# Routed experts: weight pieces of 512 columns, gate and linear columns in separate steps, second products two steps behind

## The chip, the core and the metric

The kernel runs on one core of a Trainium2 chip. The metric is the device time of one execution, in microseconds (us); it is given as the median of three runs. Five engines run their own instruction streams: PE (TensorE, matrix products), ACT (ScalarE), DVE (VectorE), POOL (GpSimd) and SP (SyncE, which here issues the large transfers). They wait for each other through semaphores. PEld is PE's loading of the stationary operand. The transfers of all queues share 16 DMA engines.

## The reference

Two layers on 512 tokens of width 1024: a state-space mixer with a dense SwiGLU, then an attention layer with eight routed SwiGLU experts, of which each token uses two. The change touches the experts alone:

```python
def _swiglu(x, w_in, w_out):
    g, u = jnp.split(x @ w_in, 2, axis=-1)        # w_in: 1024 x 7168, gate columns, then linear columns
    return (jax.nn.silu(g) * u) @ w_out           # w_out: 3584 x 1024

def _moe_swiglu(x, w_router, w_in, w_out):
    logits = (xf @ w_router).astype(jnp.float32)
    top_val, top_idx = lax.top_k(logits, TOP_K)   # two of eight experts per token
    gate = jax.nn.softmax(top_val, axis=-1)
    ...
    # each expert's tokens are gathered, go through _swiglu, and are added back times their gate
```

The layer ends with `LayerNorm(ALPHA * x + experts)`.

## The kernel before

The stage of the experts follows the router. The eight experts are ranked by how many tokens chose them; the code is built for fixed token counts by rank ("caps": 160, 148, 136, 132, 132, 128, 116, 112 in the version that runs here). Phases of one or two ranks follow each other: 4, then 0 and 7, then 1 and 6, then 3, then 2 and 5. Within a phase of two the chunks of both alternate; the last ten chunks of the stage are all of rank 5.

An expert's 3584 hidden columns are cut into 14 **chunks** of 256, so the stage has 112 chunks. A chunk needs three **pieces** of weights of 1 MB each, as float32: its 256 gate columns of the first matrix (all 1024 rows), its 256 linear columns, and its 256 rows of the second matrix. In memory a row's 256 columns are a run of 1 KB; a row of the second matrix is a run of 4 KB. `moe_load` issues the pieces from SP in the order gate, linear, second matrix, into six buffers `mraw`; the two pieces of the first chunk go into the two halves of `X`, which is free by then (`ahead`).

All products are made of float16 pairs. `moe_conv` has ACT write the high half of a piece (L1127), `moe_lo` has DVE write the low half (L1133) and then, since the buffer is free, issues the load six pieces later. The halves go to `wi` (first matrix, two buffers) or `woh`/`wol` (second matrix, three). `mm3` turns each product into three matmuls: high by high (L277), high by low (L278), low by high (L279).

A step `i` of the loop in `moe` has `moe_in(i, 0)` and `moe_in(i, 1)`, which make 128 columns each of the hidden width: eight row blocks times gate and linear, three matmuls each, in one bank of PSUM (`gu`, three banks). ACT makes `hs` = silu(gate) from the bank (L1150), DVE multiplies by the linear half (`hf`, L1151), rounds to `hh` (L1154) and subtracts for `hl` (L1155). Then `moe_out(i - 1)` multiplies the previous chunk's `hh`, `hl` with its second matrix into `y`. Per chunk that is 96 matmuls of cap columns for the first matrix, and for the second 48 of cap columns, or 12 of 512 columns where the cap is at most 128.

Between these, `fill` slips in pieces of other work: the gathering of the next phase's tokens (`dispatch`, L1077), the places of the rows (`where`), the transposed results of finished experts (`moe_rows`), and, in the last chunks, `moe_sum`: POOL loads the accumulated rows back from `XD` (L1232, four transfers of 512 KB, and one gather L1234), and the layer norm of all rows begins, shared by ACT, DVE and POOL (`STEPS`). `finish` adds the last expert and writes out. [...]

At the stage's beginning SP reads eight registers from `order` (L2205), the experts' numbers, then issues the first two pieces. While these load, PE gathers the first expert's tokens. POOL loads the gamma and beta of the last layer norm, broadcast to all partitions (`load_gb(1, 1)`, 512 KB written by each of two transfers).

## Time and profile before

| | |
|---|---|
| median of three runs | 1831.0 us (1829.42 to 1831.13) |
| the profiled execution, its own time | 1829.31 us |
| its span (first to last instruction) | 1827.5 us |
| PE busy / PEld busy | 1686.7 us / 1324.2 us |
| DVE busy / ACT busy / POOL busy | 1393.8 / 1003.0 / 220.5 us |
| moved by DMA over the span | 433.69 MB, 237 GB/s |

The stage of the experts runs from about 777 us to 1804 us of the span. "Busy" counts the time in which an engine has an instruction under way; matmuls overlap, so a busy PE need not be at its peak. The mean granted clock of TensorE over the span was 0.965 of full speed.

### The profile page before, as it was taken

Reading aid. Unit: us, or ns where it says so; the run is one execution under the profiler, and the core shown is the slowest. Engines: PE = TensorE matmul, PEld = TensorE weight load, DVE = VectorE, ACT = ScalarE, POOL = GpSimd, SP = SyncE. Lnnn points to the kernel's source line nnn. Section 1 sums busy time; section 2 is a strip of 40 time slices with the busy share of each in tenths; the row PEclk is TensorE's granted clock in tenths of the full one; section 3 lists DMA queues with packets and bytes.
Section 4 is the critical chain, followed back from the end, with each engine's and each line's share of the span. In section 5 each row is a group of like instructions: output and inputs, shape, how many; then the busy total and the mean of one; then the engine's idle time right before and its main releaser. Section 6 shows DMA issues by size and latency. Waiting matters only on the chain.

```text
span 1827.5 us, 45045 instructions
## 1 busy us (share of the span) xinstructions
PE 1686.7 (92%) x19531; PEld 1324.2 (72%) x19531; DVE 1393.8 (76%) x2049; ACT 1003.0 (55%) x1100; POOL 220.5 (12%) x232
## 2 busy tenths in 40 slices
PE   4689999999999888879999999999999999999974
PEld 4455464444445554579999999999999899999863
DVE  9873653333246685569999999999999899999987
ACT  4223333232232573267767766767777677777771
POOL 6920100000000200100000012120000100000125
PEclk7889999999999999789999999999999999999997
DMA  4236423432342000199999999999999999999991
GB/s 82 53 96 220 128 70 93 115 93 93 119 144 93 24 24 15 44 357 379 361 343 340 354 357 355 347 359 347 379 368 364 303 373 378 371 384 376 369 361 62
DMA packets 359320, 433.69 MB, mean 237 GB/s; under 512 B 30480, under 2 KB 321384, under 8 KB 359104
## 3 DMA queue, kind: packets, MB, share of 16 engines
q1 hardware_dynamic: 346832, 417.55, 67.2%
q0 software_dynamic: 3984, 12.56, 2.4%
q8 instruction: 156, 2.56, 0.6%
q10 hardware_dynamic: 8288, 0.54, 0.3%
q14 instruction: 60, 0.49, 0.1%
HBM read 416.81 MB, written 11.17 MB: 234 GB/s over the span
## 4 chain that ended last, share of the span: by engine, by line
PE 71%; DVE 16%; DMA 5%; ACT 4%; issue 3%; POOL 1%; SPq 0%; DVEq 0%; ACTq 0%; POOLq 0%
PE gu L277 9%; PE gu L279 9%; PE gu L278 9%; PE ps L278 7%; PE ps L279 7%; PE ps L277 7%; PE y L277 5%; PE y L279 5%; PE y L278 5%; DVE wi L1133 4%; DMA mraw<-in_moe_w_in_dram 3%; DVE wol L1133 2%; DMA mraw<-in_moe_w_out_dram 2%; PE glu L279 1%; PE glu L277 1%
## 5 line engine op out<-in xcount | busy, mean ns | idle before, releaser
L279 PE MATMUL gu<-xe,wi 128*128 128x132 f16 (+6 forms) x3584 | 635.4, 222 | 21.9 <-DVE wi L1133 21.8
L277 PE MATMUL gu<-xe,wi 128*128 128x132 f16 (+6 forms) x3584 | 635.5, 222 | 8.9 <-ACT wi L1127 4.5
L278 PE MATMUL gu<-xe,wi 128*128 128x132 f16 (+6 forms) x3584 | 635.4, 221 | 0.0
L1133 DVE SCALAR_TENSOR_TENSOR wi<-mraw,wi 128x2048 f16<-128x2048 f32 x222 | 507.3, 2285 | 5.9 <-ACT wi L1127 5.5
L1127 ACT ACTIVATE wi<-mraw 128x2048 f16<-128x2048 f32 x222 | 419.1, 1906 | 63.4 <-DMA mraw<-in_moe_w_in_dram 58.7
L279 PEld LDWEIGHTS <-wi 128*128 128x128 f16 x3584 | 350.3, 98 | 24.3 <-DVE wi L1133 24.2
L278 PEld LDWEIGHTS <-wi 128*128 128x128 f16 x3584 | 352.7, 98 | 9.5 <-issue 4.9
L277 PEld LDWEIGHTS <-wi 128*128 128x128 f16 x3584 | 350.8, 98 | 8.5 <-ACT wi L1127 4.7
L1133 DVE SCALAR_TENSOR_TENSOR wol<-mraw,woh 128x2048 f16<-128x2048 f32 x112 | 255.8, 2284 | 0.3 <-ACT woh L1127 0.3
L1127 ACT ACTIVATE woh<-mraw 128x2048 f16<-128x2048 f32 x112 | 213.5, 1906 | 22.9 <-DMA mraw<-in_moe_w_out_dram 22.6
L278 PE MATMUL y<-hl,woh 128*128 128x132 f16 (+3 forms) x1120 | 209.5, 225 | 0.0
L279 PE MATMUL y<-hh,wol 128*128 128x132 f16 (+3 forms) x1120 | 209.5, 225 | 0.0
L277 PE MATMUL y<-hh,woh 128*128 128x132 f16 (+3 forms) x1120 | 209.4, 225 | 0.0
L1150 ACT ACTIVATE hs<-gu 128x132 f32<-128x132 f32 (+4 forms) x224 | 62.2, 278 | 195.5 <-PE gu L279 195.3
L105 DVE SCALAR_TENSOR_TENSOR wf<-raw,wf 128x2048 f16<-128x2048 f32 x34 | 77.8, 2292 | 95.7 <-ACT wf L104 95.7
L277 PE MATMUL ps<-xt,wf 128*128 128x512 f16 x320 | 121.3, 379 | 0.0
L278 PE MATMUL ps<-xt,wf 128*128 128x512 f16 x320 | 121.3, 379 | 0.0
L279 PE MATMUL ps<-xt,wf 128*128 128x512 f16 x320 | 121.3, 379 | 0.0
L1185 POOL DMA_INDIRECT XD<-yr,at x12 | 24.8, 2066 | 787.8 <-ACT yr L1218 438.1
L277 PEld LDWEIGHTS <-woh 128*128 128x128 f16 x1120 | 109.6, 98 | 0.0
L279 PEld LDWEIGHTS <-wol 128*128 128x128 f16 x1120 | 109.6, 98 | 0.0
L278 PEld LDWEIGHTS <-woh 128*128 128x128 f16 x1120 | 109.5, 98 | 0.1
(471 smaller groups left out, 2746.7 us busy)
## 6 DMA issues: line engine op xcount, KB each, us to landing
mraw<-in_moe_w_in_dram SPq DMA_DIRECT2D x222, 1024.0 KB
mraw<-in_moe_w_out_dram SPq DMA_DIRECT2D x112, 1024.0 KB
raw<-in_ffn_w_in_dram SPq DMA_DIRECT2D x44, 512.0 KB
raw<-in_ffn_w_out_dram SPq DMA_DIRECT2D x11, 1024.0 KB
raw<-in_s_w_glu_dram SPq DMA_DIRECT2D x64, 128.0 KB
raw<-in_mla_o_w_dram SPq DMA_DIRECT2D x4, 1024.0 KB
XD<-X SPq DMA_DIRECT2D x5, 512.0 KB
xj<-in_x_dram SPq DMA_DIRECT2D x4, 512.0 KB
```

The costliest lines, as they stand in the source:

```text
L105: nc.vector.scalar_tensor_tensor(lo[:, c], raw[:, c], scale[j], hi[:, c], op0=OP.mult, op1=OP.subtract)
L277: mm(out, lh, rh, start=first, stop=False, **kw)
L278: mm(out, lh, rl, start=False, stop=False, **kw)
L279: mm(out, ll, rh, start=False, stop=last, **kw)
L1127: nc.scalar.activation(hi, raw, AF.Copy, scale=WS)
L1133: self.nc.vector.scalar_tensor_tensor(lo, raw, WS, hi, op0=OP.mult, op1=OP.subtract)
L1150: nc.scalar.activation(sg, p[:, :cap], AF.Silu, scale=1.0 / (WS * XS))
L1185: self.nc.gpsimd.indirect_dma_start(out=self.XD, out_offset=bass.IndirectOffsetOnAxis(ap=self.at[:n, j:j + 1], axis=0), in_=yr[:n], in_off ...
```

## The change

Two neighbouring chunks of an expert now share their weights' columns differently. `MOE` lists pairs: entry `(r, 2c)` is a step for the **gate** columns of 512 hidden columns, `(r, 2c + 1)` one for the **linear** columns. A piece of the first matrix is 512 columns by half of the 1024 rows (runs of 2 KB, still 1 MB); a piece of the second matrix is as before.

- `moe_in(i, half)` makes 256 columns of one kind in one bank. In a gate step ACT writes silu of two caps' width into `hs` and keeps it. In the linear step DVE makes `hf`, `hh`, `hl` of that width. The number and shape of the matmuls stay.
- The second matrix's pieces come one step later in the order of loads and conversions (`piece`), and `moe_out(i - 2)` takes the place of `moe_out(i - 1)`, except at the end of the last phase's two parts.
- The second matrix has four buffers: two tiles `wo` and the two halves of `X`.
- At the beginning SP reads one register, issues the first two pieces, and reads the other seven afterwards. The two pieces of the second step are issued ahead of the first piece of the second matrix; `moe_load(9)` issues all six buffers' loads at once (before: `moe_load(6)`, four).
- `load_gb(1, 1)` moves from the router to the first step of `moe_sum`.

```diff
-MOE = [rc for ph in PLAN for rc in sorted(((r, c) for c in range(NCH) for r in ph),
-       key=...)]
+MOE = [(r, 2 * c + v) for ph in PLAN for r, c in sorted(((r, c) for c in range(NCH // 2) for r in ph),
+       key=...)
+       for v in range(2)]
...
-            self.load_gb(1, 1)
...
             if part < 2:
-                nc.sync.dma_start(t.rearrange("p (k f) -> p k f", k=KD),
-                                  wi[:, bass.ds(e, 1), :, part, c * CH:(c + 1) * CH].rearrange("p o k f -> p (o k) f"))
+                n, k = 2 * CH, KD // 2
+                nc.sync.dma_start(t.rearrange("p (k f) -> p k f", k=k),
+                                  wi[:, bass.ds(e, 1), part * k:(part + 1) * k, c % 2, c // 2 * n:(c // 2 + 1) * n]
+                                  .rearrange("p o k f -> p (o k) f"))
...
+    def piece(self, i, part):
+
+        i -= part == 2
+        return (i if 0 <= i < NE * NCH else None), part
...
-    def moe_in(self, i, ft):
+    def moe_in(self, i, half):
...
+        for part in range(2):
+            for a in range(2):
+                for k in range(kh):
+                    s = k * 2 * CH + (2 * half + a) * 128
...
+                    self.mm3(p[:, a * cap:(a + 1) * cap], wih[:, part, s], wil[:, part, s], xh[:, kk], xl[:, kk],
+                             kk == 0 and a == 0, kk == KD - 1, skip_group_check=True)
...
+        if c % 2 == 0:
+            sg = self.hp.tile([128, w], F, name="hs", tag="hs", bufs=4)[:, :2 * cap]
+            nc.scalar.activation(sg, p[:, :2 * cap], AF.Silu, scale=1.0 / (WS * XS))
+            self.sg[i + 1, half] = sg
+            return
...
-        self.mh[i, ft] = (hh, hl)
+        self.mh[i - 1 + half] = (hh, hl)
...
+        self.load_gb(1, 1)
         acc = [t.bitcast(F).rearrange("p (t d) -> p t d", t=2) for t in self.xf]
...
+        self.wo = [self.op.tile([128, 2, 2 * D], H, name=f"wo{i}", bufs=1) for i in range(2)]
+        self.wo += [t.bitcast(H).rearrange("p (a n) -> p a n", a=2) for t in self.ahead]
...
-        self.moe_load(6)
+        self.moe_load(9)
...
-            if i > 0:
-                self.moe_out(i - 1)
+            for j in [i - 2] * (i > 1 and i - 2 not in (others, tot - 1)) + [i - 1] * (i - 1 in (others, tot - 1)):
+                self.moe_out(j)
...
+        expert(RANKS[0])
...
         self.moe_load(2, True)
+        for r in RANKS[1:]:
+            expert(r)
```

How the instructions stand on SP where the stage begins, before (`X` receives the first two pieces, `mraw` the others; 128x8x256 is 128 partitions by eight row blocks by 256 columns; ISA sets a register):

```order
L2205 TENSOR_LOAD order x8
L1106 ISA
L1106 DMA X<-in_moe_w_in_dram 128x8x256
L1106 ISA
L1106 DMA X<-in_moe_w_in_dram 128x8x256
L2213 TENSOR_LOAD close_fit
L2216 COMPARE_AND_BRANCH
L1109 ISA
L1109 DMA mraw<-in_moe_w_out_dram 128x2x1024
L1106 ISA
L1106 DMA mraw<-in_moe_w_in_dram 128x8x256
```

and now:

```order
L2236 TENSOR_LOAD order
L1111 ISA
L1111 DMA X<-in_moe_w_in_dram 128x4x512
L1111 ISA
L1111 DMA X<-in_moe_w_in_dram 128x4x512
L2236 TENSOR_LOAD order x7
L2247 TENSOR_LOAD close_fit
L2250 COMPARE_AND_BRANCH
L1111 ISA
L1111 DMA mraw<-in_moe_w_in_dram 128x4x512
L1111 ISA
L1111 DMA mraw<-in_moe_w_in_dram 128x4x512
```

Seven of the eight register loads moved behind the first two pieces, and two pieces of the first matrix stand where the first piece of the second matrix stood.

On DVE, one chunk in the first phase before (`wi`, `wol` are low halves of weights; `hf`, `hh`, `hl` the hidden values):

```order
L1133 SCALAR_TENSOR_TENSOR wi<-mraw,wi 128x2048
L1151 SCALAR_TENSOR_TENSOR hf<-gu,hs 128x132
L1154 CAST hh<-hf 128x132
L1155 TENSOR_TENSOR hl<-hf,hh 128x132
L1133 SCALAR_TENSOR_TENSOR wi<-mraw,wi 128x2048
L1151 SCALAR_TENSOR_TENSOR hf<-gu,hs 128x132
L1154 CAST hh<-hf 128x132
L1155 TENSOR_TENSOR hl<-hf,hh 128x132
L1133 SCALAR_TENSOR_TENSOR wol<-mraw,woh 128x2048
```

and now a gate step and a linear step, that is two chunks' worth (`wo_6291` and `wo_6292` are the two tiles `wo`; in the next two steps `X` stands there):

```order
L1145 SCALAR_TENSOR_TENSOR wi<-mraw,wi 128x2048 x2
L1145 SCALAR_TENSOR_TENSOR wo_6291<-mraw,wo_6291 128x2048
L1145 SCALAR_TENSOR_TENSOR wi<-mraw,wi 128x2048
L1172 SCALAR_TENSOR_TENSOR hf<-gu,hs 128x264
L1175 CAST hh<-hf 128x264
L1176 TENSOR_TENSOR hl<-hf,hh 128x264
L1145 SCALAR_TENSOR_TENSOR wi<-mraw,wi 128x2048
L1172 SCALAR_TENSOR_TENSOR hf<-gu,hs 128x264
L1175 CAST hh<-hf 128x264
L1176 TENSOR_TENSOR hl<-hf,hh 128x264
L1145 SCALAR_TENSOR_TENSOR wo_6292<-mraw,wo_6292 128x2048
```

Six small instructions of double width stand for twelve, and all of them stand in the linear step.

On POOL, where the last rows are added to `XD` and the layer norm begins, now:

```order
L1207 DMA XD<-yr,at 640x1024 x9
L201 DMA gb<-in_ln_g_dram 128x1024
L201 DMA gb<-in_ln_b_dram 128x1024
L1255 DMA xfh<-XD 128x1024 x2
L1255 DMA xfl<-XD 128x1024 x2
L1257 DMA va<-XD,at 128x1024
```

Before, the two `gb` transfers stood ahead of all of the stage's work on POOL, and the row behind the adds was the first read of `XD`.

## Rows read from the trace of the kernel before

**Rows 1.** Windows: stretch, us, engines' busy us (instructions), PEclk, DMA share, GB/s

```profile
777.00:840.00 63.00, 51.12 (x758) 49.90 (x759) 48.68 (x59) 41.67 (x37) 3.87 (x8) 0.88 1.03 366
840.00:1735.00 895.00, 885.63 (x13838) 844.99 (x13836) 841.94 (x1040) 640.04 (x578) 62.09 (x42) 1.00 1.04 360
1735.00:1804.00 69.00, 55.09 (x670) 42.70 (x667) 60.36 (x84) 40.89 (x46) 28.57 (x15) 0.98 0.71 261
```

**Rows 2.** The same view, 70 us with one expert, cap 132, no dispatch

```profile
1490.00:1560.00 70.00, 70.00 (x1215) 70.00 (x1212) 68.05 (x76) 52.94 (x47) 0.00 (x0) 1.00 1.07 382
```

**Rows 3.** Timeline of DVE, one chunk: start us, us, instruction

```profile
1617.52 2.28 DVE L1133 SCALAR_TENSOR_TENSOR wol<-mraw,woh 128x2048 f16<-128x2048 f32 x1
1619.73 2.28 DVE L1133 SCALAR_TENSOR_TENSOR wi<-mraw,wi 128x2048 f16<-128x2048 f32 x1
1621.93 0.29 DVE L1151 SCALAR_TENSOR_TENSOR hf<-gu,hs 128x136 f32<-128x136 f32 x1
...
1622.74 2.28 DVE L1133 SCALAR_TENSOR_TENSOR wi<-mraw,wi 128x2048 f16<-128x2048 f32 x1
...
1625.75 2.28 DVE L1133 SCALAR_TENSOR_TENSOR wol<-mraw,woh 128x2048 f16<-128x2048 f32 x1
```

**Rows 4.** Instruction groups of one shape: busy us, mean ns, idle before

```profile
L1155 DVE TENSOR_TENSOR hl<-hf,hh 128x160 f16<-128x160 f32 x28 | 9.2, 330 | 1.0
L1155 DVE TENSOR_TENSOR hl<-hf,hh 128x112 f16<-128x112 f32 x28 | 7.8, 279 | 1.0
```

**Rows 5.** Timeline of ACT at the stage's start; [idle before <-releaser]

```profile
783.28 0.50 ACT L1083 ACTIVATE xe<-gu 128x396 f16<-128x396 f32 x1 [1.34 <-PE gu L1077]
786.28 1.91 ACT L1127 ACTIVATE wi<-X 128x2048 f16<-128x2048 f32 x1 [2.50 <-DMA X<-in_moe_w_in_dram]
789.62 1.91 ACT L1127 ACTIVATE wi<-X 128x2048 f16<-128x2048 f32 x1 [1.43 <-DMA X<-in_moe_w_in_dram]
792.19 1.91 ACT L1127 ACTIVATE woh<-mraw 128x2048 f16<-128x2048 f32 x1 [0.66 <-DMA mraw<-in_moe_w_out_dram]
795.20 1.91 ACT L1127 ACTIVATE wi<-mraw 128x2048 f16<-128x2048 f32 x1 [1.10 <-DMA mraw<-in_moe_w_in_dram]
```

**Rows 6.** Chain that ended last, 774 to 790: start us, us, what

```profile
774.48 0.49 SPq L2205
...
777.52 0.41 SPq L1106
```

**Rows 7.** Timeline of POOL: its first transfer issued at the stage's start

```profile
777.70 0.60 POOL L199 DMA_DIRECT2D gb<-in_ln_g_dram  x1 [0.30 <-issue]
```

**Rows 8.** PE's waits, 777 to 840: total us, times, longest us

```profile
PE gu L279 <- DVE wi L1133: 6.8, 4, 3.8
PE gu L277 <- ACT wi L1127: 4.5, 1, 4.5
```

**Rows 9.** Windows again: seven us behind the first weight matmul

```profile
789.00:796.00 7.00, 4.91 (x45) 4.64 (x46) 5.68 (x3) 4.62 (x3) 0.00 (x0) 0.52 1.08 360
```

**Rows 10.** PE's waits, 840 to 1735

```profile
PE gu L277 <- ACT yr L1218: 3.5, 1, 3.5
PE gu L1077 <- DVE hf L1151: 2.7, 2, 2.2
```

**Rows 11.** Timeline of ACT: the longest wait for weights in mid-stage

```profile
1453.82 1.91 ACT L1127 ACTIVATE wi<-mraw 128x2048 f16<-128x2048 f32 x1 [7.52 <-DMA mraw<-in_moe_w_in_dram]
```

**Rows 12.** PE's waits, 1735 to 1804

```profile
PE gu L279 <- DVE wi L1133: 13.4, 6, 4.3
```

**Rows 13.** Timeline of ACT near the stage's end

```profile
1742.67 1.91 ACT L1127 ACTIVATE wi<-mraw 128x2048 f16<-128x2048 f32 x1 [3.87 <-DMA mraw<-in_moe_w_in_dram]
1747.60 1.91 ACT L1127 ACTIVATE woh<-mraw 128x2048 f16<-128x2048 f32 x1 [2.85 <-DMA mraw<-in_moe_w_out_dram]
```

**Rows 14.** Timeline of DVE near the stage's end

```profile
1776.88 2.47 DVE L1155 TENSOR_TENSOR hl<-hf,hh 128x128 f16<-128x128 f32 x1
```

**Rows 15.** Timeline of POOL near the stage's end

```profile
1776.85 2.35 POOL L250 TENSOR_TENSOR xfh<-xfh,gb 128x1024 f32<-128x1024 f32 x1
```

More of the change, by code (lines that the diff above doesn't have):

```diff
@@ L1096, in moe_load @@
         wo = self.A["moe_w_out"][0].rearrange("e (f p) d -> p e f d", p=128)
-        while self.nload < min(upto, 3 * NE * NCH):
-            i, part = divmod(self.nload, 3)
+        while self.nload < min(upto, 3 * NE * NCH + 3):
+            i, part = self.piece(*divmod(self.nload, 3))
+            self.nload += 1
+            if i is None:
+                continue
             r, c = MOE[i]
@@ L1112, in moe_load @@
                 self.mraw[i, part] = t
-            self.nload += 1
+    def piece(self, i, part):
+        i -= part == 2
+        return (i if 0 <= i < NE * NCH else None), part
     def moe_conv(self, i, part):
         nc = self.nc
-        if i >= NE * NCH:
+        n = 3 * i + part
+        i, part = self.piece(i, part)
+        if i is None:
             return
@@ L1122, in moe_conv @@
             w = [w[:, 0], w[:, 1]]
-            w += [self.op.tile([128, 2 * D], H, name=n, tag=n, bufs=3) for n in ("woh", "wol")]
+            w += self.wo[i % 4]
             self.mw[i] = w
@@ L1127, in moe_conv @@
         nc.scalar.activation(hi, raw, AF.Copy, scale=WS)
-        self.mlo.append((3 * i + part, lo, raw, hi))
+        self.mlo.append((n, lo, raw, hi))
     def moe_lo(self):
@@ L1142, in moe_in @@
         p = self.gbank()
[L1143 to L1153 removed]
+        kh = KD // 2
+        for part in range(2):
+            for a in range(2):
+                for k in range(kh):
+                    s = k * 2 * CH + (2 * half + a) * 128
+                    s = slice(s, s + 128)
+                    kk = part * kh + k
+                    self.mm3(p[:, a * cap:(a + 1) * cap], wih[:, part, s], wil[:, part, s], xh[:, kk], xl[:, kk],
+                             kk == 0 and a == 0, kk == KD - 1, skip_group_check=True)
+        w = 2 * max(CAPS)
+        if c % 2 == 0:
[3 more added lines that the diff above has]
+            return
+        h = self.hp.tile([128, w], F, name="hf", tag="hf", bufs=2)[:, :2 * cap]
+        nc.vector.scalar_tensor_tensor(h, p[:, :2 * cap], HS / (WS * XS), self.sg.pop((i, half)), op0=OP.mult, op1=OP.mult)
+        hh = self.hp.tile([128, w], H, name="hh", tag="hh", bufs=4)[:, :2 * cap]
+        hl = self.hp.tile([128, w], H, name="hl", tag="hl", bufs=4)[:, :2 * cap]
         nc.vector.tensor_copy(hh, h)
         nc.vector.tensor_sub(hl, h, hh)
[L1156 removed]
+        self.mh[i - 1 + half] = (hh, hl)
     def moe_out(self, i):
@@ L1167, in moe_out @@
         y = self.y[r]
+        th, tl = self.mh.pop(i)
         for ft in range(2):
-            hh, hl = self.mh.pop((i, ft))
+            hh, hl = (t[:, ft * cap:(ft + 1) * cap] for t in (th, tl))
             first, last = c == 0 and ft == 0, c == NCH - 1 and ft == 1
@@ L1280, in moe @@
         tot = len(MOE)
-        self.mraw, self.mw, self.mh, self.ys, self.mlo, self.y = {}, {}, {}, {}, [], {}
+        self.mraw, self.mw, self.mh, self.ys, self.mlo, self.y, self.sg = {}, {}, {}, {}, [], {}, {}
         self.nload = 2
+        self.wo = [self.op.tile([128, 2, 2 * D], H, name=f"wo{i}", bufs=1) for i in range(2)]
+        self.wo += [t.bitcast(H).rearrange("p (a n) -> p a n", a=2) for t in self.ahead]
+        self.wo = [[t[:, a] for a in range(2)] for t in self.wo]
         self.mraw = {(0, part): self.ahead[part] for part in range(2)}
-        self.moe_load(6)
+        self.moe_load(9)
         for r in PLAN[0]:
@@ L1339, in moe @@
                 fill(i, 1)
[L1340 to L1342 removed]
+            for j in [i - 2] * (i > 1 and i - 2 not in (others, tot - 1)) + [i - 1] * (i - 1 in (others, tot - 1)):
+                self.moe_out(j)
+                r, c = MOE[j]
                 if c == NCH - 1 and r != LAST:
@@ L2204, in run, with expert @@
         keep, late = self.route(self.lg)
-        self.ereg = [nc.values_load(self.order[0:1, r:r + 1], engines=[mybir.EngineType.SP], min_val=0, max_val=NE - 1,
-                                    skip_runtime_bounds_check_because="a sum of at most one index under 8")
-                     for r in range(NE)]
+        self.ereg = {}
+        def expert(r):
+            self.ereg[r] = nc.values_load(self.order[0:1, r:r + 1], engines=[mybir.EngineType.SP], min_val=0, max_val=NE - 1,
+                                          skip_runtime_bounds_check_because="a sum of at most one index under 8")
+        expert(RANKS[0])
         self.ahead = [self.X[:, 2 * i:2 * i + 2].rearrange("p t d -> p (t d)") for i in range(2)]
```

14 lines of the change are left out of this document (1 added, 13 removed).

## The prediction

> **What bounds the kernel now.** I began with the page's table of slices and saw that PE and DVE are both nearly full from 777 us on, where the experts run, and that DMA is too. Three resources near their limit say little by themselves, so I asked for busy time by stretch [rows 1]. The stage falls in three. From 777 to 840 PE is busy 51.12 of 63.00 us, from 840 to 1735 885.63 of 895.00, from 1735 to 1804 55.09 of 69.00. PE is idle 11.9, 9.4 and 13.9 us, 35.2 in all. What the reader should see is how little that is: no change that keeps the matmuls can win much more than these 35 us, however much it takes from DVE or DMA.
>
> That holds only if a busy PE is a PE at its pace. [...] A chunk of that expert has 96 + 48 matmuls, so PE needs 144 x 57.6 = 8.3 us for it. DVE shows 8.23 us from one `wol` to the next [rows 3], and almost no gap. The third price is the transfer. At the stage's start ACT waits for each piece, so its starts are landings: the second matrix's piece came 2.57 us after the one ahead of it (789.62 to 792.19), the next piece of the first matrix 3.01 us later (to 795.20) [rows 5]. A chunk of two such and one such costs 2 x 3.01 + 2.57 = 8.6 us of DMA there. Three clocks of 8.2 to 8.6 us per chunk: PE sets the end, and the other two have no lead with which to cover a hiccup. The change leaves the PE clock alone and lowers the two others.
>
> [...]
>
> **The change part by part.**
>
> *DVE's small instructions.* `hl` takes 330 ns at 160 columns and 279 at 112 [rows 4]: 51/48 = 1.06 ns per column, and 279 - 112 x 1.06 = 160 ns fixed. A pair of chunks has twelve such instructions (`hf`, `hh`, `hl` four times); now six of double width. If the other two kinds have a like fixed part, that is 6 x 0.16 = 0.96 us less per pair, less what neighbouring instructions overlap: the group of three takes 0.81 us now (1621.93 to 1622.74) [rows 3], at double width 0.81 + 136 x (1.06 to 3.2 ns for one to three instructions, whose widths partly overlap) = 0.95 to 1.24. I take 1.2. A pair then costs DVE six conversions at 2.21 us (1617.52 to 1619.73) plus two groups, 13.3 + 2.4 = 15.7 us, against 2 x 8.23 = 16.5 now. Over 56 pairs that is 45 us of DVE time, off the path as long as PE sets the pace, so its worth is 0 in itself; it buys DVE some 0.9 us of lead on PE (16.6 us) per pair. ACT saves the same way (one silu of double width for two) and waits for PE in gate steps only; nothing there is on the path.
>
> *Pieces with runs of 2 KB.* The trace has runs of 1 KB (3.01 us) and 4 KB (2.57). A piece of 1 MB is 1024, 512 or 256 runs; with a constant price per run, (3.01 - 2.57)/768 = 0.57 ns, a piece of 512 runs takes 2.57 + 256 x 0.00057 = 2.72 us. The bounds are the rows themselves, 2.57 and 3.01. A chunk's transfers fall from 8.6 to 2 x 2.72 + 2.57 = 8.0 us, 0.3 below PE. Off the path too; what it buys is that the six buffers of `mraw` fill up and stay full.
>
> [...]
>
> *The stage's beginning.* From SP's first register to its first issue are 3.04 us (774.48 to 777.52) [rows 6]; eight reads, the first 0.49. The 2.55 behind it hold the seven that now stand behind the two issues, and the first issue's set-up, so the issues come about 2.3 us earlier. POOL's `gb` transfers, issued at 777.70 [rows 7] beside the first weights, write 1 MB; at the piece's price that is 2.6 to 3.0 us which the first two pieces no longer share. Together they land some 5 us earlier, about 781 and 784.5. But the first conversion then waits for ACT's own `xe` (783.28 + 0.50 = 783.8) [rows 5] instead of the landing at 786.28, so 2.5 us are won, no more: conversions end at 785.7 and 787.6, DVE's low halves (2.28 each) at 788.0 and 790.3 instead of about 790.5 and 793.8. Then the second step: before, its pieces came behind the second matrix, the first at 795.20, so its second near 798; now they are third and fourth, landed near 790, and no longer waited for. PE's waits in this stretch are 6.8 us on DVE's low halves, the longest 3.8, and 4.5 on ACT's first conversion [rows 8]. Of these 11.3 I keep 2.0 of the 4.5 (783.8 + 1.9 against PE's end of the gathering near 783.7), 2.3 for the first low half and up to 0.7 for the second, in sum 5, so 6.3 are won. [...] Term: **6** won, bounds 4 to 9.
>
> *The middle.* The idle 9.4 us hold one stall of 3.5 us behind ACT's `yr`, 2.7 on DVE's `hf` for a free bank [rows 10], and some 3 in small ones. The 3.5 began with DMA: ACT had stood 7.52 us for a piece [rows 11], and `yr` stood in its queue behind that conversion. That hiccup comes back, but now with the buffers full: six pieces of 2.7 us are 16 us of cover against 7.5. The 2.7 go with DVE's lead. Against it stands the linear step: DVE has three conversions and all the small work there, 6.6 + 2.4 = 9.0 us, against PE's 8.3, so it falls 0.7 behind and makes it up in the gate step (6.6). Conversions run one step ahead of PE's need, so 0.7 should be covered. Term: **5** won, bounds 4 lost to 9 won.
>
> *The end.* 13.9 us idle, of which PE waits 13.4 on low halves [rows 12]. Two causes: the reads of `XD` take DMA, and ACT waits 3.87 and 2.85 us for pieces [rows 13]; and DVE stands while POOL works: `hl`, 0.28 to 0.33 us elsewhere [rows 4], takes 2.47 [rows 14], ending where a POOL instruction of 2.35 us does [rows 15]. The first part, 6 of the 13.9, is now covered by full buffers, though `gb` adds 1 MB (2.6 to 3.0 us) just ahead of these reads: four times 512 KB, a gather of as much, and 1 MB are 3.5 MB, 9.5 us, against 16 of cover. If the buffers aren't full, the 3 us of `gb` are a loss. On POOL's queue the two issues (0.60 each) stand ahead of the reads, which wait for the row adds anyway. The second part, about 7, stays where it hits; half as many small instructions can be hit, each still for the rest of a POOL instruction, and DVE has 0.4 us more lead per chunk. I take 3 of 7. Term: **9** won, bounds 3 lost to 13 won. The 24 us behind the stage are unchanged.
>
> **Sum.** 6 + 5 + 9 = 20 us. The profiled execution took 1829.3 (span 1827.5), so it would take 1809.3; the median of the runs is 1831.0, which the same 20 bring to 1811. I say 1810. By the bounds alone, from the median: 31 won gives 1800, 3 lost 1834, but the three worst cases don't come together.
>
> **The rivals.**
>
> *Runs of 2 KB transfer no faster.* Then DMA keeps 8.6 us per chunk, the buffers never fill, the 3.5 stall stays and `gb` adds 3 us to the end: 6 from the beginning, 2 from the middle, 3 from DVE at the end, minus 3: 8 won, 1823. For it: in the steady stretch DMA moves 382 GB/s [rows 2], more than a piece at 3.01 us (348). Against it: rows 5.
>
> *DVE, not PE, sets the pace.* Then all 45 us of DVE's savings come out beside the 6 of the beginning, 1831 - 51 = 1780. Against it: 57.6 ns per matmul [rows 2].
>
> *All idleness goes but the first wait.* 31 won, 1800.
>
> *The gains are given back*, in the order of the layer norm's last pieces or by `gb`: 1829 to 1832.
>
> *Slower: the linear step's burst reaches PE.* If the lead of the conversions (two `wi` buffers, so the first conversion for a step can't start before PE left the step two ahead) is below 0.7 us, PE waits 0.7 us in each of 56 pairs, 39 us, against 6 + 9 won elsewhere: 1831 + 39 - 15 = 1855. It decides at that lead. Against it: a step's first half is converted during the step ahead of it (8.3 us), and needs 1.9 + 2.3.
>
> **How the numbers follow.** Forecast, 1803 to 1817: 0.60. No faster transfers, 1817 to 1825: 0.20. All idleness gone, 1797 to 1803: 0.07. DVE's pace: 0.03. Given back: 0.05. Slower: 0.05. The range takes in the first three: 1797 to 1825. A measurement of this kernel tells 0.2% (3.7 us) from no change. Faster by more: 0.60 + 0.20 + 0.07 + 0.03 less 0.02 for the edge, 0.88. Within: 0.07. Slower: 0.05.
>
> **What would show it.** PE idle by the three stretches near 5, 4 and 5 us; landings 2.7 us apart for pieces of the first matrix; ACT hardly waiting for pieces after the first; the first low half near 788; DVE with 45 us less to do and more gaps. Wrong would be: PE waits on low halves spread evenly over the linear steps (the slower rival), a pitch other than 57.6 ns, or the waits for pieces as before.

## The result, and the profile after

| | before | after |
|---|---|---|
| median, us | 1831.04 (1829.42 to 1831.13) | 1812.62 (1811.57 to 1814.98) |
| ratio, with its 95% interval | | 0.9902 (0.989 to 0.9915) |
| the profiled execution's own time / its span, us | 1829.31 / 1827.5 | 1811.57 / 1809.8 |
| PE busy, us | 1686.7 | 1685.9 |
| DVE busy, us (instructions) | 1393.8 (2049) | 1350.3 (1713) |
| DMA packets / share of the 16 engines taken by SP's queue | 359,320 / 67.2% | 244,630 / 65.2% |

The change wins 18.4 us by the medians and 17.7 by the profiled executions. PE is as busy as it was and DVE has 43.5 us less to do; that so little of these 43.5 came out is the first thing to see.

The stage now ends at 1786.1 instead of 1803.6 us, so the stretches of [rows 1] no longer hold equal work. To compare them, both traces are cut at the stage's own beginning and end, at 840, and some 85 us ahead of the end. The stretches do not hold exactly the same matmuls (758 and 938 in the first), so what is compared is PE's idle time. Windows of the kernel before, cut so (columns as in [rows 1]):

```profile
777.56:840.00 62.44, 51.12 (x758) 49.90 (x759) 48.34 (x58) 41.67 (x37) 3.65 (x7) 0.88 1.04 370
840.00:1717.00 877.00, 867.63 (x13606) 830.64 (x13604) 826.37 (x1022) 626.91 (x565) 58.09 (x38) 1.00 1.04 360
1717.00:1803.60 86.60, 73.09 (x904) 57.05 (x901) 75.55 (x101) 53.62 (x59) 32.57 (x18) 0.98 0.79 282
```

The same view of the changed kernel:

```profile
776.65:840.00 63.35, 59.18 (x938) 58.03 (x939) 56.06 (x49) 48.02 (x37) 2.33 (x4) 0.94 1.04 399
840.00:1701.00 861.00, 858.55 (x13456) 822.16 (x13454) 779.50 (x722) 607.19 (x462) 68.87 (x39) 1.00 1.01 364
1701.00:1786.10 85.10, 72.54 (x873) 57.02 (x870) 72.97 (x75) 53.50 (x50) 28.91 (x20) 0.94 0.76 285
```

PE's idle time is the stretch less PE's busy time: 11.3, 9.4 and 13.5 us before, 4.2, 2.5 and 12.6 after. So 7.15 us were won at the beginning, 6.92 in the middle and 0.95 at the end, together 15.0. The stage also begins 0.9 us earlier (776.65 against 777.56), and PE was busy 1.6 us less over the whole of it; its granted clock was 0.94 instead of 0.88 in the first stretch, but 0.94 instead of 0.98 in the last. These are the 17.5 us by which the stage ends earlier. Neither of these two is shown to come from the change. Experiments 5 and 6 have the same code up to there, and their first matmul of the stage (L1078) starts at 776.5 and 779.6 us. And experiments 5, 6 and 8, again with the same code up to there, have granted clocks of 0.95, 0.89 and 0.93 from 777 to 840.

What answers to [rows 2], a window of 70 us of the changed kernel with one expert of cap 132 and no gathering:

```profile
1480.00:1550.00 70.00, 70.00 (x1211) 70.00 (x1209) 65.81 (x51) 52.58 (x40) 0.00 (x0) 1.00 1.04 391
```

1211 matmuls in 70.00 us are 57.8 ns each, against 57.6: PE goes at the pace it had, while DVE is down from 68.05 to 65.81 us.

What answers to [rows 5], the timeline of ACT at the stage's start after:

```profile
782.36 0.50 ACT L1084 ACTIVATE xe<-gu 128x396 f16<-128x396 f32 x1 [1.23 <-PE gu L1078]
782.75 3.70 ACT L1139 ACTIVATE wi<-X 128x2048 f16<-128x2048 f32 x2
786.35 1.90 ACT L1139 ACTIVATE wi<-mraw 128x2048 f16<-128x2048 f32 x1
788.80 1.91 ACT L1139 ACTIVATE wi<-mraw 128x2048 f16<-128x2048 f32 x1 [0.55 <-DMA mraw<-in_moe_w_in_dram]
```

The first two conversions (the row with x2) stand right behind `xe`, the third behind them, and only the fourth waits for its landing, 0.55 us. PE's waits from 777 to 840, as [rows 8] before:

```profile
PE gu L281 <- DVE wi L1145: 2.0, 1, 2.0
PE gu L279 <- ACT wi L1139: 1.9, 1, 1.9
```

3.9 us instead of 11.3. PE's waits from 840 to 1700, as [rows 10]:

```profile
PE gu L1078 <- DVE hf L1172: 1.2, 1, 1.2
PE gu L281 <- DVE wi L1145: 0.9, 1, 0.9
```

The wait behind `yr`, 3.5 us before, is gone. ACT's waits for pieces in the same stretch show why, before (840 to 1717):

```profile
ACT wi L1127 <- DMA mraw<-in_moe_w_in_dram: 46.8, 54, 7.5
ACT woh L1127 <- DMA mraw<-in_moe_w_out_dram: 16.2, 27, 2.9
```

and now (840 to 1700):

```profile
ACT wi L1139 <- PE gu L281: 112.7, 44, 3.8
...
ACT wi L1139 <- DMA mraw<-in_moe_w_in_dram: 13.1, 14, 6.3
...
ACT wo L1139 <- DMA mraw<-in_moe_w_out_dram: 3.7, 5, 1.7
ACT X L1139 <- DMA mraw<-in_moe_w_out_dram: 2.1, 4, 0.6
```

So 46.8 + 16.2 us of waiting for pieces have become 13.1 + 3.7 + 2.1, and ACT waits 112.7 us for PE to give back a buffer `wi`: the pieces are mostly there before they are wanted.

Last, PE's waits from 1717 to 1750 and from 1750 to 1790, as [rows 12]:

```profile
PE gu L281 <- DVE wi L1145: 4.2, 2, 2.4
PE gu L279 <- ACT wi L1139: 0.8, 1, 0.8
```

```profile
PE gu L281 <- DVE wi L1145: 7.5, 3, 4.3
```

12.5 us, against 13.4 in [rows 12]. This is the part that did not follow the forecast.

### The profile page after: what moved, and what is told of

Same layout as the page of the kernel before. It is cut to its first block, busy times and chain, and to the rows that moved or that the text cites. A ratio compares the mean times of both kernels' runs of the same rounds, so it can differ in the third digit from the quotient of the medians.

```text
span 1809.8 us, 44600 instructions
## 1 busy us (share of the span) xinstructions
PE 1685.9 (93%) x19531; PEld 1324.6 (73%) x19531; DVE 1350.3 (75%) x1713; ACT 987.7 (55%) x988; POOL 224.4 (12%) x232
## 2 busy tenths in 40 slices
DMA packets 244630, 433.69 MB, mean 240 GB/s; under 512 B 30480, under 2 KB 92008, under 8 KB 244416
## 3 DMA queue, kind: packets, MB, share of 16 engines
q1 hardware_dynamic: 232144, 417.55, 65.2%
## 4 chain that ended last, share of the span: by engine, by line
PE 77%; DVE 13%; issue 3%; ACT 3%; DMA 2%; POOL 1%; POOLq 0%; DVEq 0%; SPq 0%; ACTq 0%
PE gu L279 10%; PE gu L281 10%; PE gu L280 10%; PE ps L280 7%; PE ps L281 7%; PE ps L279 7%; PE y L279 5%; PE y L281 5%; PE y L280 5%; DVE wi L1145 2%; PE gu L1078 2%; PE glu L279 1%; PE glu L281 1%; PE glu L280 1%; DMA mraw<-in_moe_w_in_dram 1%
## 5 line engine op out<-in xcount | busy, mean ns | idle before, releaser
L281 PEld LDWEIGHTS <-wi 128*128 128x128 f16 x3584 | 350.3, 98 | 16.5 <-DVE wi L1145 16.5
L281 PE MATMUL y<-hh,X 128*128 128x132 f16 (+3 forms) x800 | 152.9, 226 | 0.0
L280 PE MATMUL y<-hl,X 128*128 128x132 f16 (+3 forms) x800 | 152.9, 226 | 0.0
L279 PE MATMUL y<-hh,X 128*128 128x132 f16 (+3 forms) x800 | 152.9, 226 | 0.0
L1145 DVE SCALAR_TENSOR_TENSOR X<-mraw,X 128x2048 f16<-128x2048 f32 x56 | 128.0, 2286 | 6.9 <-ACT X L1139 6.8
L1145 DVE SCALAR_TENSOR_TENSOR wo<-mraw,wo 128x2048 f16<-128x2048 f32 x56 | 130.2, 2325 | 1.1 <-ACT wo L1139 0.9
L1139 ACT ACTIVATE wo<-mraw 128x2048 f16<-128x2048 f32 x56 | 106.6, 1904 | 7.0 <-DMA mraw<-in_moe_w_out_dram 7.0
L1139 ACT ACTIVATE X<-mraw 128x2048 f16<-128x2048 f32 x56 | 106.6, 1904 | 5.3 <-DMA mraw<-in_moe_w_out_dram 5.3
L106 ACT ACTIVATE wf<-raw 128x2048 f16<-128x2048 f32 x34 | 64.5, 1900 | 76.9 <-PE ps L281 42.2
L1168 ACT ACTIVATE hs<-gu 128x264 f32<-128x264 f32 (+6 forms) x112 | 43.7, 390 | 107.2 <-PE gu L281 107.1
```

The costliest lines, as they stand in the source:

```text
L106: nc.scalar.activation(hi[:, c], raw[:, c], AF.Copy, scale=scale[j])
L279: mm(out, lh, rh, start=first, stop=False, **kw)
L280: mm(out, lh, rl, start=False, stop=False, **kw)
L281: mm(out, ll, rh, start=False, stop=last, **kw)
L1139: nc.scalar.activation(hi, raw, AF.Copy, scale=WS)
L1145: self.nc.vector.scalar_tensor_tensor(lo, raw, WS, hi, op0=OP.mult, op1=OP.subtract)
```

## The experiments

Four theories stood at the start: (A) shorter transfers fill the buffers; (B) DVE's wider instructions give it a lead; (C) the beginning is won by the order of the registers, `gb` and the pieces; (D) the end is held by two things of its own, transfers around 1700 to 1730 and POOL's share of the layer norm. The rivals were that one of the two leads is worth nothing alone, and for the end that `gb`'s new place, or the chain of small DVE instructions of the norm, is what stands there.

**1. Runs of 1 KB** (the changed kernel; a piece is 256 columns by all 1024 rows again):

```diff
-                n, k = 2 * CH, KD // 2
-                nc.sync.dma_start(t.rearrange("p (k f) -> p k f", k=k),
-                                  wi[:, bass.ds(e, 1), part * k:(part + 1) * k, c % 2, c // 2 * n:(c // 2 + 1) * n]
+                nc.sync.dma_start(t.rearrange("p (k f) -> p k f", k=KD),
+                                  wi[:, bass.ds(e, 1), :, part, c * CH:(c + 1) * CH].rearrange("p o k f -> p (o k) f"))
```

> The changed kernel, but a piece of the first matrix is loaded as 256 columns by all 1024 rows, in runs of 1 KB, as before the change; the products of the first matrix are then of the wrong columns, the work is the same. Theory A (the full buffers, which the longer runs fill, are what took the stalls out of the middle): ACT waits for pieces again in most steps, PE idle from 840 us to the end of the last phase's first part goes from 2.5 us back towards 9.4, the end loses 2 more, in all 5 to 9 us more than the changed kernel's 1812.6, so 1818 to 1822, ratio to before 0.993 to 0.995. Theory B (DVE's lead took them out): the waits for pieces come back but PE's idle time stays within 2 us of 2.5, ratio 0.990 to 0.991. If a run of 2 KB transferred no faster than one of 1 KB, nothing at all would change.

Measured: 1820.6 us (1819.4 to 1822.7), ratio to before 0.9945 (0.9929 to 0.9962), 8.0 above the changed kernel. ACT's waits from 840 to 1700:

```profile
ACT wi L1137 <- DMA mraw<-in_moe_w_in_dram: 61.9, 65, 7.4
ACT X L1137 <- DMA mraw<-in_moe_w_out_dram: 13.8, 18, 2.3
ACT wo L1137 <- DMA mraw<-in_moe_w_out_dram: 10.0, 16, 1.7
```

85.7 us for pieces instead of 18.9, so 2 KB runs do transfer faster. By how much, the packets' time shows: those of SP's queue take 67.6% of 1817.6 us here and 65.2% of 1809.8 in the changed kernel, 49 us over 224 pieces of the first matrix, an estimate of 0.22 us per piece. From 1712 to 1732, where DMA moves other transfers too, the core moves 393 GB/s here at a DMA share of 1.05, and 404 in the changed kernel at 1.04. PE's idle time from 840 to 1700 went only from 2.5 to 4.3 us and at the beginning by some 1.3; most of the 8 us stands at the end, where PE waits 16.5 us instead of 12.5 (1700 to 1790) and runs at a granted clock of 0.92 instead of 0.94. The full buffers are worth more at the end than in the middle.

**2. Small instructions of single width** (`hf`, `hh`, `hl` in two halves each, the rest as changed):

```diff
-        nc.vector.scalar_tensor_tensor(h, p[:, :2 * cap], ..., self.sg.pop((i, half)), ...)
-        nc.vector.tensor_copy(hh, h)
-        nc.vector.tensor_sub(hl, h, hh)
+        for a in range(2):
+            s = slice(a * cap, (a + 1) * cap)
+            nc.vector.scalar_tensor_tensor(h[:, s], p[:, s], ..., sg[:, s], ...)
+            nc.vector.tensor_copy(hh[:, s], h[:, s])
+            nc.vector.tensor_sub(hl[:, s], h[:, s], hh[:, s])
```

> The changed kernel, with each of DVE's hf, hh, hl of two caps' width cut into two of one cap's, which gives DVE back six instructions per pair of chunks, 0.85 to 1 us. Theory A (DMA's lead): no change, PE idle in the middle within 2 us of 2.5, ratio 0.990 to 0.991. Theory B (DVE's lead): PE idle in the middle rises by 3 to 6 us and the end by 1 to 2, ratio 0.992 to 0.994. If DVE set the pace, the whole 45 us would come back, ratio 1.01.

Measured: 1820.1 us (1819.2 to 1821.2), ratio 0.9938 (0.9921 to 0.9954), 7.5 above the changed kernel. PE's longest wait from 840 to 1700:

```profile
PE gu L1078 <- DVE hf L1177: 3.1, 1, 3.1
```

DVE does 32 us more than the changed kernel's 778.5 in the same 860, and PE is idle 5.7 us instead of 2.5. Most of the difference is that one wait for `hf`, 3.1 us where the changed kernel waits 1.2, at a place where the gathering for the next phase adds work to DVE. From 1170 to 1230, around it, the granted clock is 0.97, and 1.00 in the changed kernel, which is another 1.8 us. In the 64 us from 776 it is 0.89 instead of 0.93, some 2 us, with 0.7 more of idle time. These four make up some 8 of the 9.3 us between the two profiled executions; the 2 us are not shown to be the edit's, since experiments 5, 6 and 8, with one code there, are as far apart (0.95, 0.89 and 0.93 from 777 to 840). So a lead of DVE is worth what it covers at such places, not the 32 us. Runs 1 and 2 together: each of the two leads, taken away alone, costs some 8 us; neither stands in for the other.

**3. `gb` back at the router** (`load_gb(1, 1)` where it was before, the rest as changed):

> The changed kernel with the gb transfers (1 MB) back where they stood, beside the first weights. Theory: the first two pieces land 2.6 to 3 us later, but the first conversion then waits some 1 to 2.5 us for them, so the start loses 1 to 2.5 us of PE time; the end has 1 MB less to move ahead of the reads of XD and PE's idle time there falls by 0 to 3 us. In sum within 2.5 us of the changed kernel either way. Rival (the transfers never cost the start anything, because ACT's xe is what the first conversion waits for): start the same, end 0 to 3 us better.

Measured: 1813.25 us (1811.2 to 1815.9), ratio 0.9903 (0.9887 to 0.992): no difference. The beginning loses (PE idle 3.4 us longer, with 1.0 on `hf` and 1.6 more on low halves) and the first half of the end wins: PE waits 2.3 instead of 5.0 us from 1717 to 1750, and 8.2 instead of 7.5 from 1750 to 1790. So the 1 MB of `gb` cost PE 3.4 us at the one place and 2.7 at the other; DMA's share was above 1 at both (1.03 and 1.04).

**4. All eight registers first** (`expert(r)` for all ranks ahead of the first issue):

> The changed kernel with all eight registers read ahead of the first two issues, as before. Theory: the first two pieces are issued and land 2.2 us later; in the changed kernel the first conversion starts right behind ACT's xe with the piece already there, the slack being unknown, so the start loses 0 to 2.2 us of PE time. Rival (the slack is over 2.2 us): nothing.

Measured: 1815.0 us (1812.7 to 1815.8), ratio 0.9907 (0.9891 to 0.9924). In the 64 us from 776 PE is idle 0.7 us longer. Its granted clock is 0.89 there instead of 0.93, which is not shown to be the registers' doing: experiment 2 leaves them as changed and has 0.89 too. The times are 2.4 us apart with spreads that overlap, and do not settle even the sign.

**5. `gb` in the second phase** (`self.load_gb(1, 1)` at step 14, meant to run after the beginning):

> The changed kernel with the gb transfers issued in mid-stage, when step 14 is reached, away from the beginning and from the end. Theory (at the end, 1 MB less in front of the reads of XD): PE's first three waits of the end, 1.0 + 2.5 + 2.0 us between 1731 and 1739, shrink to 0 to 3 us in all, as they did with gb at its old place, and the start keeps its gain: 2 to 4 us below the changed kernel's 1812.6. Rival (the transfer displaces the weights wherever it stands): the same 1812.6 within 1.5.

Measured: 1812.56 us (1810.3 to 1817.0), ratio 0.9904 (0.9883 to 0.9925). The run did not test what it was made for. Timeline of POOL:

```profile
776.65 0.60 POOL L201 DMA_DIRECT2D gb<-in_ln_g_dram  x1 [21.59 <-DVE sel L1056]
```

POOL issued it at 776.65 us, the stage's very beginning, though 14 steps of the loop stand ahead of it in the code; nothing that POOL had to do before it waited for one of these steps. It is a second run of experiment 3, with its waits: 7.0 us in all at the beginning, 2.0 and 7.8 at the end.

**6. A quarter of `XD` read back** (as 5, and the four reads take 256 of 1024 columns, so that the norm works on partly stale rows):

```diff
-            nc.gpsimd.dma_start(acc[tt], self.XD[tt * 128:(tt + 1) * 128])
+            nc.gpsimd.dma_start(acc[tt][:, :256], self.XD[tt * 128:(tt + 1) * 128, :256])
```

> As gb_mid, and the four reads of XD at the end fetch 256 of the 1024 columns, 0.5 MB instead of 2; the layer norm's other columns are not the right ones. Theory (the end's first waits come from transfers that take the DMA engines from the weights): these waits go to under 1 us, ACT no longer waits for pieces there, 1 to 3 us below gb_mid. The second group of waits, 4.5 + 2.7 + 0.8 us from 1757 on, stays. Rival (all of the end's waits come from DVE): no change against gb_mid.

Measured: 1808.53 us (1807.5 to 1811.5), ratio 0.9874 (0.9857 to 0.989). The window 1717 to 1750:

```profile
1717.00:1750.00 33.00, 33.00 (x457) 27.34 (x455) 30.92 (x35) 27.86 (x26) 10.65 (x9) 1.00 1.04 401
```

PE is never idle there: these waits were DMA's. The profiled execution took 1811.5 us, as long as that of experiment 5, since its stage began 3.1 us later (779.6 against 776.5); so the 4.0 us between the medians are not read from this one trace. From 1750 to 1780 it waits 8.9 us, more than the 7.5 of the changed kernel, so part of what the first gave was lost in the second.

**7. No POOL work for the first two token blocks** (their scaling, gamma and beta left out, the rows written unfinished):

```diff
         def early(tt):
-            norm(tt, 0)
-            end(tt, 0)
+            nc.sync.dma_start(self.out[0, tt * 128:(tt + 1) * 128], acc[tt])
```

> The changed kernel without POOL's six large instructions on the first two blocks of tokens at the end (scale, times gamma, plus beta); these rows are written out unfinished. Theory (DVE is held while POOL works): no hh, hl or low half takes more than its usual time, the second group of PE's waits, 8.0 us from 1757 on, goes to under 2, 5 to 8 us below the changed kernel, so 1805 to 1808. Rival (DVE is behind because of its own root chain of 2.4 us and the late pieces): 4 or more of the 8.0 stay.

Measured: 1802.22 us (1801.7 to 1803.7), ratio 0.984 (0.9824 to 0.9857), 10.4 below the changed kernel (the profiled executions are 7.9 apart). PE's waits 1717 to 1790, and DVE's `hl` of the first linear step behind the norm's root:

```profile
PE gu L281 <- DVE wi L1145: 3.6, 2, 2.2
PE gu L279 <- ACT wi L1139: 1.1, 1, 1.1
```

```profile
1754.45 0.42 DVE L1176 TENSOR_TENSOR hl<-hf,hh 128x256 f16<-128x256 f32 x1
```

The waits of the first half stay (4.7 us), those of the second are gone altogether, although the chain of small DVE instructions is still there. `hl` takes 0.42 us where it took 2.54. So the second half is POOL's work, and the rival (the chain) falls.

**8. The scaling on ACT** (as 5, and `norm(tt, 1)` in `early`, which takes one of three large instructions per block from POOL):

> As gb_mid, and the scaling of the first two blocks of tokens at the end, 3.2 and 1.2 to 5.6 us on POOL, is made by ACT (1.2 us each, as it makes the other two blocks). Theory (each POOL instruction can hold one or two of DVE's): two of six POOL instructions are gone, so a third of the 8.0 us goes, 2 to 3 us below gb_mid; ACT has the room (33 of 69 us busy). Rival (ACT's in-order queue holds the conversions behind the scaling, which waits for the root): no gain or 1 to 2 us lost.

Measured: 1811.78 us (1809.6 to 1812.9), ratio 0.989 (0.9873 to 0.9906); not separable from experiment 5. DVE at the end:

```profile
1759.26 2.00 DVE L1175 CAST hh<-hf 128x256 f16<-128x256 f32 x1
1761.29 2.54 DVE L1176 TENSOR_TENSOR hl<-hf,hh 128x256 f16<-128x256 f32 x1
...
1765.96 8.79 DVE L1145 SCALAR_TENSOR_TENSOR wi<-mraw,wi 128x2048 f16<-128x2048 f32 x2
```

Four large POOL instructions are left instead of six (for each block, 2.35 and 2.41 us at their shortest), so a third of them is gone, but a fifth of their time (2.4 of 11.9 us). They find others to hold: `hh` 2.00, `hl` 2.54, and two conversions, 8.79 us for both instead of 4.5. PE's waits behind 1750 are 7.2 us against 7.8 in experiment 5.

**9. `gb` behind the row adds of a phase** (at step 70, where a row add that waits stands ahead of it in POOL's queue):

> The changed kernel with the gb transfers issued at step 70, behind the row adds of three earlier experts on POOL's queue, so that POOL cannot reach them at the beginning, as it did in gb_mid. Theory: the start is the changed kernel's (4.2 us of PE idle), the middle is the same within 1 us, and the end is gb_mid's (first waits 2 to 4 us instead of 5.5): 2 to 3 us below 1812.6, about 1810. Rival (the transfer displaces weights wherever it stands): 1812.6 within 1.5, with the loss in the middle.

Measured: 1811.83 us (1809.1 to 1816.4), ratio 0.9902 (0.9883 to 0.9921). POOL issued it at 1271 us, behind row adds issued at 1252.2 and 1269.2, so this is the place that experiment 5 wanted. The beginning keeps its 2.0 + 1.9 us of waits. At the end PE waits 2.2 us instead of 5.0 from 1717 to 1750, and 8.4 instead of 7.5 from 1750 to 1790: of the 2.8 us won two remain, which the times (0.8 apart, spread of 7) cannot show.

**10. Two of the reads half a step later each** (as 9):

```diff
-        for tt in range(TT):
+        for tt in range(2):
             nc.gpsimd.dma_start(acc[tt], self.XD[tt * 128:(tt + 1) * 128])
...
-        for _ in range(WAIT):
+        for k in range(WAIT):
             yield
+            if k < 2:
+                nc.gpsimd.dma_start(acc[k + 2], self.XD[(k + 2) * 128:(k + 3) * 128])
```

> As gb_late, and of the four reads of XD at the end two are issued later, one in each of the next two half steps, with the scaling of the gathered rows moved behind them. Theory (the first waits of the end are a matter of how many bytes stand ahead of the weights at once): the first waits fall to 0 to 2 us, 1808 to 1810, the lowest time of the kernels that compute everything. Rival (the same bytes take the same DMA time, later): as gb_late within 1.

Measured: 1811.34 us (1809.3 to 1813.5), ratio 0.989 (0.9874 to 0.9907). PE waits 1.9 us in the first half and 10.0 in the second. It is the lowest median of all kernels that do the whole work, 1.3 us below the changed kernel, and within the spread of both: no version was found that is shown to beat it.

**11. Second products one step behind** (`moe_out(i - 1)` for every step):

```diff
-            for j in [i - 2] * (...) + [i - 1] * (i - 1 in (others, tot - 1)):
+            for j in [i - 1] * (i > 0):
```

> The changed kernel with the second products one step behind instead of two, the rest the same. Theory (the second step of distance buys that PE never waits for hl or for the second matrix): in linear steps PE reaches the second product of the gate chunk 2.7 us after the half that it is made of, DVE needs a conversion of 2.3 and the three small instructions of 1.2 in that time, so PE waits up to 1 us in most of the 56 pairs and at phase changes more: 1820 to 1860, with rows of PE waiting at y on DVE's hl. Rival (DVE's lead covers it): within 2 us of 1812.6.

Measured: 1812.63 us (1811.9 to 1816.4), ratio 0.9906 (0.989 to 0.9923): no difference. From 1717 to 1790 PE waits 4.9 us for `hh`, 3.3 for the second matrix and 2.0 for `hl`: the waits change their place, from the first products to the second, and sum to 10.2 us. In the middle `hh` and `hl` cost 1.1 us. The two steps of distance buy nothing that can be measured.

**12. The kernel before, with the registers and `gb` alone** (one register ahead of the first issue, `gb` at step 70; pieces, steps and widths as before):

> The kernel before with two of the beginning's edits alone: seven registers read behind the first two issues, and the gb transfers away from the beginning (at step 70). The order of the pieces is as before, with the second matrix ahead of the second chunk's columns. Theory (the first two pieces land early enough for ACT's xe to set the first conversion, but the second chunk's pieces still come fourth and fifth): the first conversion starts at 783.8 instead of 786.3, the wait of 3.8 us for the second chunk's low half shrinks to 1 to 2; the start gains 3 to 5 us, the rest nothing, 1826 to 1828. Rival (the start's gain needs the new order of pieces): 1 us or less.

Measured: 1825.97 us (1824.3 to 1828.3), ratio 0.9972 (0.9963 to 0.9982), 4.5 below the kernel before. ACT at the stage's start, then PE's waits from 779 to 840:

```profile
783.34 0.50 ACT L1082 ACTIVATE xe<-gu 128x396 f16<-128x396 f32 x1 [1.28 <-PE gu L1076]
783.74 3.70 ACT L1126 ACTIVATE wi<-X 128x2048 f16<-128x2048 f32 x2
...
790.71 1.91 ACT L1126 ACTIVATE wi<-mraw 128x2048 f16<-128x2048 f32 x1 [1.10 <-DMA mraw<-in_moe_w_in_dram]
```

```profile
PE gu L279 <- DVE wi L1132: 5.7, 3, 3.4
PE gu L277 <- ACT wi L1126: 1.9, 1, 1.9
```

The first conversions stand right behind `xe` (783.34), as in the changed kernel. But the third comes with `woh`, and the second step's first piece lands at 790.7, where the changed kernel has converted three pieces by 788.3. PE waits 7.6 us instead of 11.3 before and 3.9 after: of the 7 us won at the beginning, about half are these two edits. The rest comes with the new pieces, their order, and all six loads at once, which no run takes apart; in experiment 1, with the new order and 1 KB runs, PE waits 5.3 us there.

## Why the prediction was right, and where it was not

The forecast was 1810 us, a gain of 20; measured were 1812.6 and 18.4. Its terms, with what the trace and the runs gave:

| term | forecast | measured |
|---|---|---|
| the beginning | 6 (4 to 9) | 7.1 of idle time |
| PE's busy time | no term | 1.6 less over the stage, not shown to be the change's |
| the middle | 5 (-4 to 9) | 6.9 |
| the end | 9 (-3 to 13) | 0.95 |

That the sum came within 2 us is luck: the beginning and the middle gave 3.1 us of idle time more than expected, PE's shorter busy time 1.6 and an earlier start 0.9, neither of which was forecast or is shown to be the change's, and the end gave 8 less.

**PE sets the pace: right.** 57.8 ns per matmul after (1211 in 70.00 us), 57.6 before (1215 in the 70.00 us of [rows 2], whose expert is the one of 8.3 us a chunk), PE busy throughout in both. That a busy PE is a PE at its pace was the author's assumption: what such a matmul takes at the least, no run shows. What bears it out is that the count per time stayed while DVE's busy time in these 70 us fell from 68.05 to 65.81. By the rival on DVE's pace all 45 us would have come out, 1780; DVE's saving was sized rightly (43.5), and in the middle, with the faster transfers' help, no more than 6.9 us came out. What told the two apart is the count of matmuls per time.

**DVE's small instructions: right.** The three of double width at cap 132, by shape (busy us, mean ns):

```profile
L1176 DVE TENSOR_TENSOR hl<-hf,hh 128x264 f16<-128x264 f32 x28 | 12.2, 434 | 1.0
L1172 DVE SCALAR_TENSOR_TENSOR hf<-gu,hs 128x264 f32<-128x264 f32 x28 | 12.0, 428 | 9.5 <-PE gu L281 9.5
L1175 DVE CAST hh<-hf 128x264 f16<-128x264 f32 x28 | 8.3, 298 | 1.0
```

Together 1.16 us; 1.2 had been taken.

**Runs of 2 KB: right in kind, too large in size.** The forecast took 0.29 us off a piece (3.01 to 2.72), from one pair of landings; the packets' time in experiment 1 gives about 0.22. It was enough: experiment 1 refutes the first rival, which gave 1823 for "no faster": with 1 KB runs ACT waits 86 us for pieces, with 2 KB 19, and the kernel is 8.0 us faster.

**The beginning: right by its steps.** The first conversion was bound by `xe`, as forecast (783.8 there, 782.75 in the trace, with the stage 0.9 earlier); the third and fourth pieces are hardly waited for (0.55 us); the waits of PE fell to 3.9 where 5 were left. No run shows what the clock gave: granted were 0.94 from the stage's start to 840 instead of 0.88, with experiments of one code as far apart (see the result).

**The middle: right.** The stall behind `yr` is gone, and with it most of the waits for `hf`. That both leads are needed was not forecast: experiments 1 and 2 lose 1.9 and 3.2 us there with one lead each.

**The slower rival, the burst of the linear step, did not come:** PE waits 2.3 us in 860.

**The end: wrong, in both its halves.** The term said that the part due to transfers, 6 us, "is now covered by full buffers", with 9.5 us of other transfers against 16 of cover. It was not covered: 5.0 us of waits remain from 1717 to 1750. Windows of the changed kernel before and during it:

```profile
1690.00:1700.00 10.00, 10.00 (x164) 9.82 (x162) 5.99 (x7) 6.62 (x8) 0.68 (x1) 1.00 0.95 361
1700.00:1704.00 4.00, 4.00 (x74) 4.00 (x72) 3.96 (x4) 4.00 (x4) 0.90 (x1) 1.00 0.91 259
1704.00:1708.00 4.00, 4.00 (x41) 2.59 (x39) 4.00 (x3) 4.00 (x5) 0.00 (x0) 1.00 1.02 277
1712.00:1732.00 20.00, 19.96 (x255) 15.46 (x252) 12.88 (x10) 9.41 (x9) 3.15 (x5) 1.00 1.04 404
```

At 1700 the buffers look full (the share of DMA is 0.95 in the window before), but from 1700 to 1708 the core moves only 259 and 277 GB/s at a DMA share of 0.91 and 1.02. What runs then and not before are the row adds to `XD`, issued at 1699.3. The prediction put no price on them. By the rate of the 20 us from 1712 (404 GB/s) these 8 us lack 1.1 MB, an estimate; that the row adds are the cause is read from their time, no run took them away. In mid-stage the rate fell in the same way behind the adds issued at 1015, 1250, 1423 and 1564 us (to between 256 and 292 GB/s for 4 us or more), but not behind those of 1267 and 1581 (385 GB/s and more). Behind the adds at the end come `gb` (1 MB), the reads and the gather (2.5 MB). And the cover was too large: six pieces of 2.7 us are 16 us up to a landing, but PE uses a piece only after ACT's 1.9 and DVE's 2.3 us, so about 12 are left. Those 1.1 MB and 3.7 (the 3.5 of the forecast, counted in 2^20 bytes) at 404 GB/s are 11.9 us, at the edge of that; meanwhile PE goes on taking pieces nearly as fast as DMA brings them (by the forecast's estimates 8.3 us for a chunk of cap 132, against 8.0 for its transfers), so little of it is made good. This estimate explains why there was no cover to spare, not the size of the 5.0 us. What the waits are made of, the experiments show, 9 and 6 taking from it step by step: without `gb` 5.0 becomes 2.2, with a quarter of the reads 0. The sentence that a cost of `gb` is hidden if the buffers are full failed with this: its 3 us came out, and the 3 it gives at the beginning are about what it takes here.

For the second half the step was that "half as many small instructions can be hit, each still for the rest of a POOL instruction", 3 of 7 won. The changed kernel's DVE, and POOL beside it:

```profile
1753.16 0.42 DVE L1172 SCALAR_TENSOR_TENSOR hf<-gu,hs 128x256 f32<-128x256 f32 x1
1753.62 0.84 DVE L1175 CAST hh<-hf 128x256 f16<-128x256 f32 x1
1754.49 2.54 DVE L1176 TENSOR_TENSOR hl<-hf,hh 128x256 f16<-128x256 f32 x1
1756.96 4.43 DVE L1145 SCALAR_TENSOR_TENSOR wi<-mraw,wi 128x2048 f16<-128x2048 f32 x1
...
1765.28 4.45 DVE L1145 SCALAR_TENSOR_TENSOR wo<-mraw,wo 128x2048 f16<-128x2048 f32 x1
```

```profile
1754.40 2.36 POOL L252 TENSOR_TENSOR xfh<-xfh,gb 128x1024 f32<-128x1024 f32 x1
1756.83 2.41 POOL L253 TENSOR_TENSOR xfh<-xfh,gb 128x1024 f32<-128x1024 f32 x1
...
1761.45 1.18 POOL L1269 TENSOR_SCALAR xfh<-xfh,sum_e,sum_d 128x1024 f32<-128x1024 f32 x1
```

`hh` and `hl` are held as before (0.84 and 2.54 instead of 0.30 and 0.43), and now the conversion is too: 4.43 us instead of 2.28. It starts at 1756.96, just behind POOL's 1756.83; that ends at 1759.24, and 2.15 us later the conversion is done. The one at 1765.28 meets POOL's 1765.15 in the same way. In the kernel before it was POOL that was held by DVE's conversions:

```profile
1779.27 4.48 POOL L251 TENSOR_TENSOR xfh<-xfh,gb 128x1024 f32<-128x1024 f32 x1
...
1783.92 5.56 POOL L1246 TENSOR_SCALAR xfh<-xfh,sum_e,sum_d 128x1024 f32<-128x1024 f32 x1
```

and on DVE beside it:

```profile
1779.27 2.28 DVE L1133 SCALAR_TENSOR_TENSOR wi<-mraw,wi 128x2048 f16<-128x2048 f32 x1
...
1781.78 2.06 DVE L1154 CAST hh<-hf 128x128 f16<-128x128 f32 x1
```

4.48 us for an instruction that takes 2.41 in the changed kernel, and 5.56 for one that takes 1.18 where nothing holds it. What DVE loses in all can be added up from the two traces, each instruction held against its usual duration, an estimate: before, 9.2 us, in four `hh` and two `hl`; now 9.8, in two `hh`, two `hl` and the two conversions. Nothing was won there. So the number of small instructions is not what counts. POOL has about 12 us of work on these two blocks (twice 1.18 + 2.35 + 2.41, its shortest durations), and in the rows above one engine's instruction is done about its usual time after the other's has ended: the conversion of 1756.96 2.15 us after POOL's, POOL's of 1779.27 2.20 us after the conversion. Which of the two loses differs: the conversion of 1756.96, 0.13 us behind POOL's start, took 4.43 us and POOL's its 2.41, while of the two that started together at 1779.27 the conversion took its 2.28 and POOL's 4.48. With fewer small instructions the loss moved to the large ones. Experiment 7 shows the size, 10.4 us for all of it by the medians and 7.9 by the profiled executions, of which 7.5 are these waits; experiment 8, that a fifth less of POOL's time gives nothing that can be measured. The two halves are also tied: where the first was shortened alone (experiments 3, 6, 9 and 10), the second grew from 7.5 to between 8.2 and 10.0 us. Why it grows was not tested.

**What each edit is worth,** by the runs: 2 KB runs 8.0 us, double width 7.5, registers and `gb` 4.5 on the kernel before (3.3 to 6.8 by the interval of its ratio), second products two steps behind 0, `gb` alone 0. They are not terms of a sum: the first two share the stalls that they cover.

## What to carry to other kernels

A lead of an engine that does not set the pace is worth the stalls that it covers, so its price is read from the waits of the engine that does, place by place, and not from busy time. Price the end of a stage on its own, with every transfer and every instruction that runs only there, and count the cover of buffers up to the use of a piece, not its landing. And look where an instruction that is moved in the code will be issued: the `gb` transfers of experiment 5 depend on nothing and were issued at 776.65 us, 14 steps ahead of their place in the code.
